# Rolling an 8192 x 8192 array by 100 columns: long memory-to-memory DMAs in 18 shrinking steps instead of 128 equal ones, and the row heads in four stages instead of two

## The chip, the cores and the metric

The kernel runs on one core of one Trainium2 chip. The metric is device time in microseconds (us), less is better.

## The reference

```python
def setup_inputs():
    return {"x": np.random.randn(8192, 8192).astype(np.float32), "shift": 100}

def reference(x, shift):
    return np.roll(x, shift, axis=1)
```

Nothing is computed. 268 MB are read and 268 MB are written, and each row of 32 KiB moves right by 400 bytes, with its last 100 columns coming round to the front.

## The kernel before

With a shift of 100, `s` is 100, `a` is 128 (the shift rounded up) and `g` is 28. The row from column 128 on, 8,064 elements or 32,256 bytes, is copied from memory to memory directly. Each DMA takes 16 rows, one for each of the 16 DMA engines, 4 rows (128 KiB) apart; SyncE and ScalarE issue them in turn:

```python
xm = x.rearrange("(c e j) w -> c j e w", e=16, j=4)
om = out.rearrange("(c e j) w -> c j e w", e=16, j=4)
for c in range(n_rows // 64):
    for j in range(4):
        engines[j % 2].dma_start(out=om[c, j, :, a:], in_=xm[c, j, :, g:n_cols - s])
```

The first 128 columns of each row, the heads, go through SBUF on GpSimd's queue. They are read in pieces of 512, 400 and 112 bytes, put together by VectorE, and written in pieces of 512 bytes:

```python
Q, J = 4, 8
n_st = n_rows // (P * Q * J)          # 2 stages
for k in range(n_st):
    ...                               # 3 + 1 + 1 reads, 2 copies
for k, h in enumerate(tiles):
    for q in range(Q):
        nc.gpsimd.dma_start(out=ot[k, q, :, :, :a], in_=h[:, q])
```

Of the kernel before, what the change touches and what calls it, by code (L numbers as in the profile page):

```python
# [1 line left out]

# [4 lines left out]


@with_exitstack
def kernel(  # L10
    ctx: ExitStack,
    tc: tile.TileContext,
    x: bass.AP,
    shift: int,
    out: bass.AP,
):
    nc = tc.nc
    n_rows, n_cols = x.shape
    s = shift % n_cols
    a = -(-s // 128) * 128  # L20
    g = a - s
    P = nc.NUM_PARTITIONS
    engines = [nc.sync, nc.scalar]
    n_chunks = 16
    rows = n_rows // n_chunks





    xm = x.rearrange("(c e j) w -> c j e w", e=16, j=4)
    om = out.rearrange("(c e j) w -> c j e w", e=16, j=4)
    if a < n_cols:
        for c in range(n_rows // 64):
            for j in range(4):
                engines[j % 2].dma_start(out=om[c, j, :, a:], in_=xm[c, j, :, g:n_cols - s])
    if a == 0:
        return


    if a > 512:
        for i in range(n_chunks):
            r = slice(i * rows, (i + 1) * rows)
            nc.gpsimd.dma_start(out=out[r, :s], in_=x[r, n_cols - s:])
            if g > 0:
                nc.gpsimd.dma_start(out=out[r, s:a], in_=x[r, :g])
        return





    Q, J = 4, 8
    n_st = n_rows // (P * Q * J)
    reads = ctx.enter_context(tc.tile_pool(name="reads", bufs=n_st))
    heads = ctx.enter_context(tc.tile_pool(name="heads", bufs=n_st))
    xt = x.rearrange("(k p j q) c -> k q p j c", q=Q, j=J, p=P)
    ot = out.rearrange("(k p j q) c -> k q p j c", q=Q, j=J, p=P)
    tiles = []
    for k in range(n_st):  # L60
        t = reads.tile([P, Q - 1, J, a], x.dtype)
        h = heads.tile([P, Q, J, a], x.dtype)
        for q in range(1, Q):
            lead = bass.AP(tensor=x.tensor, offset=(k * P * J * Q + q) * n_cols - s,
                           ap=[[J * Q * n_cols, P], [Q * n_cols, J], [1, a]])
            nc.gpsimd.dma_start(out=t[:, q - 1], in_=lead)  # L66
        nc.gpsimd.dma_start(out=h[:, Q - 1, :, :s], in_=xt[k, Q - 1, :, :, n_cols - s:])  # L67
        nc.vector.tensor_copy(h[:, :Q - 1, :, :s], t[:, :, :, :s])  # L68
        if g > 0:
            nc.gpsimd.dma_start(out=h[:, 0, :, s:], in_=xt[k, 0, :, :, :g])  # L70
            nc.vector.tensor_copy(h[:, 1:, :, s:], t[:, :, :, s:])  # L71
        tiles.append(h)
# [5 lines that stand above are left out]
# [1 line left out]
_INS = ['x', 'shift']  # L79
_OUTS = [((8192, 8192), 'float32')]  # L80

_NUMBERS = {'shift': 100}


# [26 lines left out]
```

## Time and profile before

| What | Before |
|---|---|
| time, median of 3 runs at first | 828.16 us |
| traffic, read and written | 268.44 MB each way |
| DMA engines' time: long rows, heads | 95.0%, 4.1% |
| long packets of 32,256 bytes | 8,192, and as many 4-byte completions (packets that report that an engine has finished its part of a DMA) |
| VectorE and GpSimd busy | 0% and 2% |

Everything is in the DMA rows: how full the 16 DMA engines are (DMA), and what they move (GB/s, in one direction). A long packet is the copy of one row by one engine. The prediction below shows the lines.

Numbers of single packets are worked out from the trace's packet records, which have queue, start, duration and size of each packet. "Memory traffic" counts a long packet's bytes twice, for read and write, and a head packet's bytes once, because its other side is SBUF. For before it is 657 GB/s from 300 to 500 us.

### The profile page before, as it was taken

To read this page: it belongs to the slowest core of one execution; us is meant where nothing else is said; L and a number is where in the kernel's file an instruction comes from. 1 tells how busy PE (TensorE), PEld (TensorE's weight loads), DVE (VectorE), ACT (ScalarE), POOL (GpSimd) and SP (SyncE) were. 2 spreads that over 40 slices of the span, in tenths; PEclk is the share of its full clock that TensorE was granted. 3 is DMA by queue.
4 is the path that set the end of the run, shared out by engine and by line. 5 is a ranking of instruction groups with operands and counts; after the bars stand their busy time and mean duration, and the time that the engine had idled before them with its cause. 6 is when DMAs were issued, how large, how long until landed. Compare 5 with 4: busy or idle time off the path is not lost. (4 is left out here: it accounts for less than half of the span.)

```text
span 826.9 us, 589 instructions
## 1 busy us (share of the span) xinstructions
DVE 3.7 (0%) x4; POOL 16.1 (2%) x22
## 2 busy tenths in 40 slices
DVE  0000000000000000000000000000000000000000
POOL 3001001000000000000000000000000000000000
DMA  9999999999999999999999999999999999999997
GB/s 305 336 338 333 337 344 351 347 352 343 339 342 330 329 329 321 334 329 326 326 328 325 337 329 325 340 318 329 317 336 333 330 325 326 328 326 339 321 328 261
DMA packets 18724, 272.70 MB, mean 330 GB/s; under 512 B 8480, under 2 KB 8480, under 8 KB 10528
## 3 DMA queue, kind: packets, MB, share of 16 engines
q10 hardware_dynamic: 8192, 132.14, 47.8%
q1 hardware_dynamic: 8192, 132.14, 47.2%
q0 software_dynamic: 2336, 8.39, 4.1%
q14 instruction: 4, 0.03, 0.0%
HBM read 268.44 MB, written 268.44 MB: 649 GB/s over the span
## 5 line engine op out<-in xcount | busy, mean ns | idle before, releaser
L75 POOL DMA_DIRECT2D out_dram<-h x8 | 6.9, 955 | 92.4 <-DMA h<-in_x_dram 79.9
L66 POOL DMA_DIRECT2D t<-in_x_dram x6 | 5.4, 910 | 0.8 <-PEq L106 0.8
L68 DVE COPY h<-t 128x2400 f32<-128x2400 f32 x2 | 2.8, 1410 | 116.2 <-DMA t<-in_x_dram 116.2
L67 POOL DMA_DIRECT2D h<-in_x_dram x2 | 1.8, 882 | 15.1 <-DMA t<-in_x_dram 15.1
L70 POOL DMA_DIRECT2D h<-in_x_dram x2 | 1.8, 883 | 14.4 <-DMA t<-in_x_dram 14.4
L71 DVE COPY h<-t 128x672 f32<-128x672 f32 x2 | 1.0, 504 | 0.0
L92 POOL MEMSET const-float32-0.0<- 128x1 f32 x1 | 0.1, 98 | 0.2 <-issue 0.2
L92 POOL MEMSET const-bfloat16-1.0<- 128x1 bf16 x1 | 0.1, 101 | 0.0
L92 POOL MEMSET const-float32-1.0<- 128x1 f32 x1 | 0.1, 98 | 0.0
L92 POOL MEMSET const-uint8-127<- 128x1 uint8 x1 | 0.1, 98 | 0.0
## 6 DMA issues: line engine op xcount, KB each, us to landing
out_dram<-in_x_dram ACTq DMA_DIRECT2D x256, 504.0 KB, 12.7
out_dram<-in_x_dram SPq DMA_DIRECT2D x256, 504.0 KB, 12.7
out_dram<-h POOLq DMA_DIRECT2D x8, 512.0 KB, 97.6
t<-in_x_dram POOLq DMA_DIRECT2D x6, 512.0 KB, 65.8
h<-in_x_dram POOLq DMA_DIRECT2D x2, 400.0 KB, 84.0
h<-in_x_dram POOLq DMA_DIRECT2D x2, 112.0 KB, 81.3
```

The costliest lines, as they stand in the source:

```text
L66: nc.gpsimd.dma_start(out=t[:, q - 1], in_=lead)
L67: nc.gpsimd.dma_start(out=h[:, Q - 1, :, :s], in_=xt[k, Q - 1, :, :, n_cols - s:])
L68: nc.vector.tensor_copy(h[:, :Q - 1, :, :s], t[:, :, :, :s])
L70: nc.gpsimd.dma_start(out=h[:, 0, :, s:], in_=xt[k, 0, :, :, :g])
L71: nc.vector.tensor_copy(h[:, 1:, :, s:], t[:, :, :, s:])
L75: nc.gpsimd.dma_start(out=ot[k, q, :, :, :a], in_=h[:, q])
L92: nc = _bacc.Bacc("TRN2", target_bir_lowering=False, num_devices=1)
```

## The change

Its intent is to have long transfers while there is much to do, to save issues and completions, and short ones at the end, so that the engines finish together. The heads go in smaller portions.

```diff
-    xm = x.rearrange("(c e j) w -> c j e w", e=16, j=4)
-    om = out.rearrange("(c e j) w -> c j e w", e=16, j=4)
-    if a < n_cols:
-        for c in range(n_rows // 64):
-            for j in range(4):
-                engines[j % 2].dma_start(out=om[c, j, :, a:], in_=xm[c, j, :, g:n_cols - s])
+    xm = x.rearrange("(c e j) w -> j e c w", e=16, j=4)
+    om = out.rearrange("(c e j) w -> j e c w", e=16, j=4)
+    blocks = n_rows // 64
+    steps, c = [], 0
+    while c < blocks:
+        steps.append((c, max(1, (blocks - c) // 4)))
+        c += steps[-1][1]
+    for c, n in steps:
+        ways = 2 if c >= blocks - 4 else 1
+        edge = [a + (n_cols - a) * k // ways for k in range(ways + 1)]
+        for j in range(4):
+            for lo, hi in zip(edge, edge[1:]):
+                if lo < hi:
+                    engines[j % 2].dma_start(out=om[j, :, c:c + n, lo:hi], in_=xm[j, :, c:c + n, lo - s:hi - s])
...
-    Q, J = 4, 8
+    Q, J = 4, 4
```

## The prediction

> **What bounds the kernel now.** I read the page first for the busy shares, then the stretches of the run (busy time and DMA share by window), then the waits of SyncE, then the waits of the other engines, and last the packet records of the trace. The page's parts 2 and 3 show that no compute engine matters and that the DMA engines are never free:
>
> ```profile
> DMA  9999999999999999999999999999999999999997
> GB/s 305 336 338 333 337 344 351 347 352 343 339 342 330 329 329 321 334 329 326 326 328 325 337 329 325 340 318 329 317 336 333 330 325 326 328 326 339 321 328 261
> q10 hardware_dynamic: 8192, 132.14, 47.8%
> q1 hardware_dynamic: 8192, 132.14, 47.2%
> q0 software_dynamic: 2336, 8.39, 4.1%
> HBM read 268.44 MB, written 268.44 MB: 649 GB/s over the span
> ```
>
> The reader is to see three things. The 16 DMA engines are full in every slice but the last; 95% of their time goes to the two queues of long row pieces (the part outside the first 128 columns), 4.1% to the heads; and the rate falls from about 343 GB/s to about 327 GB/s once the heads are done. The stretches say the same more sharply:
>
> ```profile
> 0.00:6.50 6.50, 0.00 (x0) 5.42 (x10) 1.00 0.68 239
> ...
> 120.00:250.00 130.00, 0.00 (x0) 3.47 (x4) 1.00 1.00 347
> 260.00:800.00 540.00, 0.00 (x0) 0.00 (x0) 1.00 1.00 328
> 800.00:820.00 20.00, 0.00 (x0) 0.00 (x0) 1.00 0.98 323
> 820.00:827.00 7.00, 0.00 (x0) 0.00 (x0) 1.00 0.30 124
> ```
>
> The last two columns are the DMA share and GB/s. From 6.5 to 820 us the share is 0.98 or more. Only the first 6.5 us (0.68) and the last 7 us (0.30) have idle DMA engines: 0.32 x 6.5 + 0.70 x 7 = 7 us of the 827, and no change of order can win more than that at the ends.
>
> Inside the full stretch an engine is busy but not at its best. In the packet records all 8192 long packets have 32,256 bytes. The shortest take 1,193 ns, 27 GB/s for an engine, 433 GB/s for 16; after 260 us the mean is about 1,555 ns and only 17% of packets are at the minimum. At the very end, from 821.7 us on, when fewer than 12 or so engines still have work, every packet takes 1,192 to 1,194 ns. So an engine is stretched by the others, not by its own work. Counting what HBM sees (twice the long bytes, once the heads' bytes, whose other side is SBUF), 20 us bins give 640 to 670 GB/s both while the heads' writes run (120 to 250 us) and after them. The common limit is thus **memory traffic at about 655 GB/s**, and 12 engines x 27 x 2 = 649 GB/s is just where the stretching stops. The traffic is 537 MB either way; 537 / 655 = 820 us.
>
> The waits of SyncE look alarming and are not:
>
> ```profile
> SPq L36 <- DMA out_dram<-in_x_dram: 679.2, 252, 6.0
> out_dram<-in_x_dram SPq DMA_DIRECT2D x256, 504.0 KB, 12.7
> ```
>
> The queue waits 679 us because only four DMAs per queue are allowed to be in flight, eight in all; each is one row per DMA engine and lands 12.7 us after its issue. 8 rows x 1.56 us = 12.5 us, so this is queueing behind work, not latency. The full DMA share shows that the window of eight is deep enough.
>
> **What the Trainium skill says.** (1) "DMA: Bandwidth & Descriptors", section on the anatomy of one DMA, gives about 2 us of fixed time for a DMA on the software path, and its section Bandwidth asks for 1 MiB or more per DMA. Here 504 KB DMAs run with a DMA share of 1.00, so that time lies beside other DMAs' data; larger DMAs have nothing of it to win. (2) The same page, section "Queues, rings and completion order", says that an engine takes turns between queues at packet granularity and that a completion is an ordered write behind earlier writes. The trace agrees with the turns (heads' packets lie between long ones) and shows the completions as 4-byte packets of 9 ns. (3) "HBM Reference", Specifications, gives some 716 GB/s for the pair's memory; 655 is 91% of that. The trace also shows more for an instant: the second round, from 3.98 us, has 16 packets in step at about 1,275 ns, 16 x 32,256 B / 1.275 us = 405 GB/s in each direction. So the limit depends on how the streams fall on each other, not only on bytes. (4) "DMA: Bandwidth & Descriptors", section "Latency and other measured facts", has copies slow down at row pitches of 512 KiB to 8 MiB. That bears on rival B below; no run here shows it yet.
>
> **The change part by part.**
>
> Larger DMAs. Each of 128 blocks has 64 rows, 4 per DMA engine. Steps of 32, 24, 18, 13, 10, 7, 6, 4, 3, 2, 2 blocks and seven of one replace 128 steps; the last four are cut into half rows. That is 14 x 4 + 4 x 8 = 88 DMAs for 512, with 124 x 64 + 4 x 128 = 8,448 long packets. Issues fall by 424 x 0.51 us (durations in the timeline), but SyncE and ScalarE are idle in waits, so this is worth 0. Completions fall from 8,192 to 88 x 16 = 1,408: 6,784 x 9 ns / 16 = **3.8 us of engine time**. If memory is the limit, the freed time only makes the other packets longer; I count a third, -1.3 us.
>
> Looser coupling. Eight DMAs in flight now mean up to some 200 rows per engine at first. In the present kernel, long packets plus their completions fill about 15.95 of 16 engines after 260 us, 0.3% idle; that bounds what waiting for the slowest engine costs at 0.3% x 820 = 2.5 us, and it again frees engines rather than memory: -0.5 us. The same number says that engines don't differ systematically by more than a few tenths of a per cent, since otherwise the fast ones would already stall.
>
> The start. The first DMA now carries 512 pieces instead of 16. The present first packets begin between 2.14 and 3.10 us after an issue at 0.74. If engines get their lists one after another they may start further apart: +0.5 us.
>
> The end. Now the engines finish between about 822.4 and 825.5 us, then 1.4 us of closing. With half rows the last packet is 0.6 us instead of 1.2. But engines that drifted apart during the long steps have to be brought together by the short ones: -0.8 us from the pieces, +1 us for drift.
>
> Heads. Four stages of 4 rows per partition: 12 + 4 + 4 reads and 16 writes, 36 DMAs for 18, each about 0.9 us of issue on GpSimd, 16 us more on an idle engine. The pieces are still 512, 400 and 112 bytes, so packets of about 4 KB stay about as many (2,048 now). The copies double in number with half the size (1.41 and 0.50 us now), on an idle engine. The heads end at 253 us of 827; even at half the speed they would be hidden. 0 us. The only trace of them should be 16 x 18 = 288 more completion packets of 9 ns, 0.2 us of engine time.
>
> Sum: -1.3 - 0.5 + 0.5 - 0.8 + 1 = about -1 us; I round to 826 from 828.16, since the parts lean down.
>
> **The rivals.** A: the ordered completion after every row stalls the engine, and this is the 360 ns between 1,193 and 1,555. For it: completions follow each row now, and all but a sixth would go. It could bring the mean packet near 1,300 ns and the time to 700 us. Against it: the rows of the second round (1,275 ns) and of the last 4 us (1,194 ns) also have a completion each. I give it 5%; a partial effect of 20 to 50 ns a row (-10 to -25 us) some 5% more.
>
> B: the new order hits memory worse. An engine used to step through neighbouring rows of one 2 MiB block; now its successive rows on a queue lie 2 MiB apart and engines can be in different blocks. For it: the skill's remark on row pitch. Against it: at one moment the 16 engines still stand 128 KiB apart as before, and their positions inside rows are already mixed. A 3% loss would give 850 us. 6%. It could as well turn out a gain of 1 to 3%.
>
> C: drift. Without a short leash an engine could end up 10 us behind, and the end would have fewer than 12 engines for that long: +3 to +6 us, 831 to 834. Against it: the 0.3% above, and packets of slow engines speed up to 1,193 ns as soon as others run dry. 15%, still within 2%.
>
> D: heads starved between long lists of rows, so that they end last. Against it: turns are by packet; they use a third of the run now. 2%.
>
> **Range and chances.** The bulk is set by bytes and a rate that I expect to hold within 1%: +-8 us; ends and drift add -2 to +5. So 817 to 836. Faster by over 2% (under 811.6) needs A or a lucky B: 0.09. Slower by over 2% (over 844.7) needs B or D: 0.07. Within 2%: 0.84.
>
> **What would show it.** Right: GB/s near 327 in the middle slices; mean long packet 1,540 to 1,570 ns; 1,400 or so completions on the two queues; heads over by 220 to 300 us; DMA share 1.00 until about 815 us. Wrong: a long-packet mean under 1,500 ns (A, or B as a gain), over 1,600 (B as a loss), a DMA share below 0.9 for over 10 us before the end (C), heads' packets in the last quarter (D). The prediction fails if the rate of the middle moves by more than 2%, in either direction, for then memory's rate is not a constant of this copy but depends on the order of rows or on completions.

## More of the kernel before

Times that are compared were taken on the same chip, beside runs of the kernel before. The experiments' profiles are not: the one trace of the kernel before was taken apart from them, and its medians differ by about 1% between chips (821 to 831 us), so a difference of 1% between such profiles means nothing by itself.

## The result, and the profile after

| | Before | Changed |
|---|---|---|
| median of 6 runs | 827.84 us | 828.95 us |
| range | 827.28 to 828.73 | 828.24 to 829.98 |
| ratio | | 1.0013 (95%: 1.0001 to 1.0026) |

A ratio is the mean time of one kernel's fast runs over that of the other's of the same rounds, so it is not quite the ratio of the medians. The two kernels take the same time; if anything the changed one is 1 us slower. The page of the changed kernel, parts 2 and 3 (40 slices of the span; then queue, packets, MB, share of the engines' time; q1 and q10 carry the long rows, q0 the heads):

```profile
DMA  9999999999999999999999999999999999999998
GB/s 312 323 344 322 337 338 327 337 339 331 332 332 331 327 337 337 339 335 338 338 341 333 335 339 338 317 326 329 325 329 331 325 331 331 323 323 323 331 312 296
q10 hardware_dynamic: 4928, 132.12, 47.6%
q1 hardware_dynamic: 4928, 132.12, 46.9%
q0 software_dynamic: 2624, 8.39, 4.1%
HBM read 268.44 MB, written 268.44 MB: 650 GB/s over the span
```

The two hardware queues have 9,856 packets instead of 16,384, because 6,784 completions are gone and 256 packets came from the half rows. The bytes, the shares and the GB/s stay. One thing has moved: the step down in the GB/s line, which marks the end of the heads, is after slice 25 (about 520 us) and no longer after slice 12 (about 250 us). In the packet records the last head packet with data ends at 521.5 us, before at 252.2 us.

The same stretches as before (us; then VectorE and GpSimd busy, clock, DMA share, GB/s):

```profile
0.00:6.50 6.50, 0.00 (x0) 5.41 (x11) 1.00 0.69 238
...
260.00:800.00 540.00, 0.00 (x0) 7.13 (x10) 1.00 0.99 331
800.00:820.00 20.00, 0.00 (x0) 0.00 (x0) 1.00 0.94 326
820.00:827.00 7.00, 0.00 (x0) 0.00 (x0) 1.00 0.58 184
```

The start is the same (238 against 239 GB/s). In the middle 331 stands against 328, because there are still heads in it; from 600 to 780 us, where neither kernel has any, memory traffic is 653 against 657 GB/s. Near the end the share is lower than before (0.94 against 0.98) and the rate is not (326 against 323). So idle DMA engines cost nothing in that stretch. The waits of SyncE and the issues show how far the DMAs grew (issues: count, KB each, median us from issue to landing):

```profile
SPq L44 <- DMA out_dram<-in_x_dram: 680.9, 40, 80.3
...
out_dram<-in_x_dram SPq DMA_DIRECT2D x2, 16128.0 KB, 159.2
...
out_dram<-in_x_dram SPq DMA_DIRECT2D x16, 252.0 KB, 6.0
```

SyncE waits 681 us in 40 waits, where it waited 679 us in 252. The issues that were saved were never on the path.

### The profile page after: what moved, and what is told of

It is laid out like the page before. It is cut to its first block, busy times and chain, and to the rows that moved or that the text cites. A ratio compares the mean times of both kernels' runs of the same rounds, so it can differ in the third digit from the quotient of the medians.

```text
span 826.3 us, 193 instructions
## 1 busy us (share of the span) xinstructions
DVE 4.5 (1%) x8; POOL 27.3 (3%) x40
## 3 DMA queue, kind: packets, MB, share of 16 engines
q0 software_dynamic: 2624, 8.39, 4.1%
## 5 line engine op out<-in xcount | busy, mean ns | idle before, releaser
L83 POOL DMA_DIRECT2D out_dram<-h x16 | 11.6, 726 | 217.2 <-DMA out_dram<-h 118.2
L74 POOL DMA_DIRECT2D t<-in_x_dram x12 | 9.5, 794 | 65.6 <-DMA h<-in_x_dram 36.1
L78 POOL DMA_DIRECT2D h<-in_x_dram x4 | 3.0, 749 | 47.1 <-DMA t<-in_x_dram 47.1
L76 DVE COPY h<-t 128x1200 f32<-128x1200 f32 x4 | 3.1, 785 | 253.8 <-DMA t<-in_x_dram 253.8
L75 POOL DMA_DIRECT2D h<-in_x_dram x4 | 3.0, 749 | 46.2 <-DMA t<-in_x_dram 46.2
L79 DVE COPY h<-t 128x336 f32<-128x336 f32 x4 | 1.7, 425 | 0.0
```

The source lines that it names most:

```text
L74: nc.gpsimd.dma_start(out=t[:, q - 1], in_=lead)
L75: nc.gpsimd.dma_start(out=h[:, Q - 1, :, :s], in_=xt[k, Q - 1, :, :, n_cols - s:])
L76: nc.vector.tensor_copy(h[:, :Q - 1, :, :s], t[:, :, :, :s])
L78: nc.gpsimd.dma_start(out=h[:, 0, :, s:], in_=xt[k, 0, :, :, :g])
L79: nc.vector.tensor_copy(h[:, 1:, :, s:], t[:, :, :, s:])
```

## The experiments

Twelve runs were made in three calls, each call on a chip of its own. The kernel before took 821.03, 831.28 and 831.33 us in them (medians), so times of different calls are not compared, only ratios.

The theory under test is the prediction's: memory traffic at some 655 GB/s sets the time, and neither the engines nor the issues do. The rivals are that the engines' time is the limit, that two effects cancel, and that completions, drift (engines that get ahead of one another when nothing holds them together) or the order of rows matter.

The late end of the heads gave a second theory to test, the turn theory: each DMA engine takes one packet from each queue in turn, and a completion packet uses up a turn just as a long packet does.

### First call: the parts alone, and what limits

**rows_only**: the changed kernel with the old heads.

```diff
-    Q, J = 4, 4
+    Q, J = 4, 8
```

> Only the tapering long-row DMAs of the change, heads in two stages as before. Memory theory (about 655 GB/s of memory traffic sets the time, whoever issues it): 828 to 830 us, within 0.3% of before. Cancelling theory (one part of the change wins what the other loses): off by 0.5% or more, most likely faster, since completions are fewer. Turn theory of the heads (every completion packet of 4 bytes takes a turn of its own among the queues, so one row per DMA gives the heads' queue a turn per long packet and many rows per DMA a turn per two): heads end near 500 us although their DMAs are those of before. If instead the four stages slow the heads: they end near 250 us.

Measured: 820.21 us against 821.03, ratio 0.9992 (0.9974 to 1.0010).

**heads_only**: the kernel before with the new heads.

```diff
-    Q, J = 4, 8
+    Q, J = 4, 4
```

> Only the four head stages of the change, long rows in 512 DMAs as before. Memory theory: 828 us within 0.3%. Cancelling theory: off by 0.5% or more, in the other direction than rows_only. Turn theory: heads end near 250 us as before, with about 0.9 head packets per long packet between 20 and 120 us. If the four stages slow the heads: they end near 520 us.

Measured: 826.17 us against 821.03, ratio 1.0057 (1.0033 to 1.0081). That is outside what the memory theory expected, and it was repeated in the third call.

Which part moved the end of the heads is seen in the GB/s lines of the two. First rows_only (818.1 us in 40 slices), then heads_only (825.1 us):

```profile
GB/s 303 331 332 342 329 345 334 336 331 345 342 338 340 344 339 338 344 344 339 345 340 341 343 328 331 334 330 333 325 336 326 334 328 330 325 333 333 330 323 286
```

```profile
GB/s 304 329 339 335 340 345 329 333 335 344 353 338 337 332 327 330 325 333 330 328 333 328 328 339 319 336 327 330 327 328 338 326 339 328 335 333 330 336 327 263
```

With the new rows and the old heads the step is after slice 23; the last head packet with data ends at 459.5 us. With the old rows and the new heads it ends at 284.7 us. So it is mainly the long-row DMAs that slow the heads. The turn theory expected that: 0.45 head packets with data per long packet in rows_only from 20 to 120 us, 0.84 in heads_only, 0.89 in before. The four stages add the rest, in the same way: they bring 288 completion packets of their own, so the heads' queue has 2,624 packets instead of 2,336, 12% more, and the heads end 13% later, both with the old rows (284.7 against 252.2 us) and with the new (521.5 against 459.5). Counted with these completions, from 5 us to the end of the heads, there are 0.98 head packets per long packet in before and heads_only, and 0.51 in rows_only and the changed kernel; turns alone would give 1 and 0.5.

**no_heads**: the kernel before, heads taken out. Its output is wrong, which doesn't matter for the time.

```diff
-    Q, J = 4, 8
-    n_st = n_rows // (P * Q * J)
... (all of the heads' code)
+    return
```

> The kernel before without any heads; the first 128 columns stay unwritten, so the result is wrong on purpose. The heads read and write 8.4 MB of memory together and take 4.1% of the DMA engines' time. Memory theory: 8.4 MB / 655 GB/s = 13 us less, 815 us. Engine-time theory (the 16 engines' occupancy bounds, long packets have a fixed duration): 4.1% of 827 = 34 us less, 794 us.

Measured: 805.97 us against 821.03, ratio 0.9811 (0.9787 to 0.9836), which is 15.5 us less (13.5 to 17.5). The page (queues, then HBM):

```profile
q10 hardware_dynamic: 8192, 132.14, 49.6%
q1 hardware_dynamic: 8192, 132.14, 49.5%
...
HBM read 264.24 MB, written 264.24 MB: 658 GB/s over the span
```

The engines' time that the heads had used was taken up again by the long packets, whose share rose from 95.0 to 99.1%, and HBM still ran at 658 GB/s. The engine-time theory (34 us) is out. The memory theory's 13 us is just under the interval; the rest may be that traffic in before was only 639 GB/s while heads were being read (20 to 120 us) against 657 later, 2.7% of 100 us. The trace of no_heads has no such dip (659 GB/s in that stretch, 662 later). That this makes up the rest is argued, not tested.

**write_only**: the long rows written from an SBUF tile, never read from memory. Its output is wrong, which doesn't matter for the time.

```diff
-        for c in range(n_rows // 64):
-            for j in range(4):
-                engines[j % 2].dma_start(out=om[c, j, :, a:], in_=xm[c, j, :, g:n_cols - s])
+    src = ctx.enter_context(tc.tile_pool(name="src", bufs=1)).tile([P, n_cols - a], x.dtype)
+    nc.sync.dma_start(out=src[:, :], in_=x[:P, g:n_cols - s])
+    for c in range(n_rows // P):
+        engines[c % 2].dma_start(out=out[c * P:(c + 1) * P, a:], in_=src[:, :])
... (and no heads)
```

> The same long rows are written, but from one SBUF tile instead of from memory, so memory sees 264 MB instead of 528; wrong on purpose, no heads. Memory theory: packets fall to the minimum of 1193 ns, 27 GB/s an engine, and the time to 264 MB / 433 GB/s = 610 us plus ends, 610 to 640 us. A theory in which each engine is slowed by its own copy work or by completions and not by memory: packets stay near 1500 ns and the time near 800 us.

Measured: 630.41 us, ratio 0.7679 (0.7664 to 0.7693). Its stretch from 20 to 600 us (GpSimd busy, clock, DMA share, GB/s):

```profile
20.00:600.00 580.00, 0.00 (x0) 1.00 1.00 431
```

The same 16 engines, just as full, move 431 instead of 328 GB/s, with a mean packet of 1,201 ns. A full DMA share thus did not mean that engines were the limit: some 360 ns of each long packet in before (1,559 less 1,201) are not the engine's own work. This run also changed the source from memory to SBUF, and loads alone were not measured; the copies at the end of no_taper, below, show the same without that change.

### Second call: the order of rows, and the shrinking

**near_rows** and **far_rows** change only which rows the 16 engines work on together.

```diff
-    xm = x.rearrange("(c e j) w -> c j e w", e=16, j=4)
-    om = out.rearrange("(c e j) w -> c j e w", e=16, j=4)
+    xm = x.rearrange("(c j e) w -> c j e w", e=16, j=4)     # near_rows: 32 KiB apart
+    om = out.rearrange("(c j e) w -> c j e w", e=16, j=4)
+    xm = x.rearrange("(e c j) w -> c j e w", e=16, j=4)     # far_rows: 16 MiB apart
+    om = out.rearrange("(e c j) w -> c j e w", e=16, j=4)
```

> The kernel before with one change: the 16 DMA engines copy 16 neighbouring rows (32 KiB apart) at a time instead of rows 128 KiB apart. If the memory rate of about 655 GB/s does not depend on the order of rows: within 0.5% of before. If it depends on how far apart the streams stand, it moves by over 2%, in a direction that I can't tell.

Measured: 839.54 us against 831.28, ratio 1.0093 (1.0055 to 1.0131): a little slower, between the two expectations.

> The kernel before with one change: each DMA engine has its own 512 rows, so that the 16 streams stand 16 MiB apart. Rate independent of order: within 0.5%. If streams at a large power of two fall on the same parts of memory, as rival B of the prediction has it, the rate of the middle falls and the time rises by 3% or more.

Measured: 2566.5 us (runs of 2587.38, 2553.15, 2579.84 and 2211.88), against 831.28. The fastest run is 2.66 times before's median. The page of a 2,587 us run:

```profile
DMA  9999999999999999999999999999999999999999
GB/s 113 107 114 107 109 113 111 118 117 113 114 109 104 104 99 102 100 112 97 104 104 99 104 109 102 98 102 108 101 103 100 100 107 106 101 101 99 112 104 92
```

The DMA engines are as full as ever and move a third; the mean long packet takes 4,766 ns (300 to 500 us). So the rate is no constant. Only the addresses were changed here, which speaks for memory itself as the shared limit and not the way to it; that is an inference. In the change, the 16 parts of a DMA still start 128 KiB apart.

**stripes**: the 16 engines share each row.

```diff
-        for c in range(n_rows // 64):
-            for j in range(4):
-                engines[j % 2].dma_start(out=om[c, j, :, a:], in_=xm[c, j, :, g:n_cols - s])
+        xs = x[:, g:n_cols - s].rearrange("(c r) (e w) -> c e r w", r=16, e=16)
+        os = out[:, a:].rearrange("(c r) (e w) -> c e r w", r=16, e=16)
+        for c in range(n_rows // 16):
+            engines[c % 2].dma_start(out=os[c], in_=xs[c])
```

> The kernel before with one change: the 16 DMA engines share each row, 2,016 bytes apiece, 16 rows in a DMA, so that all streams read one neighbouring 32 KiB. The pieces are 16 times as many. If memory traffic alone bounds and the engines have 20% to spare (1193 against 1555 ns), the cost of a piece is hidden: within 1%. If streams that walk together collide less, as in the second round of before (405 GB/s), faster by over 2%. If the fixed cost of a piece shows, slower by over 2%.

Measured: 879.48 us, ratio 1.0574 (1.0544 to 1.0605), slower. The smallest piece takes 80 ns; 2,016 bytes at 27 GB/s would be 75, so by this estimate about 5 ns are fixed. The mean is 104 ns, 1.3 times the minimum, as for whole rows (1,555 over 1,193 ns), but in another way: half of the pieces take 82 ns or less, and one in twenty over 165. So no gain from walking together shows. Whether the fixed part or the slow pieces made this kernel slower was not separated.

The run also bears on the turn theory. The heads' DMAs are those of before, and yet the heads are over after 67 us instead of 252, because the packets beside them are short. From 20 to 60 us there are 0.53 head packets (completions included) per piece; with one completion after 16 pieces, turns alone give 17/32 = 0.53.

**no_taper**: the changed kernel with four equal steps of 32 blocks, and so without half rows.

```diff
-        steps.append((c, max(1, (blocks - c) // 4)))
+        steps.append((c, 32))
```

> The changed kernel without its shrinking steps: four steps of 32 blocks, 16 long DMAs in all, so that nothing holds the engines together. Drift theory (rival C): engines drift apart by more than they do in the changed kernel, where up to one of 16 is idle from 660 us on; the end with fewer than 12 engines lasts several us and the time is 3 to 10 us above the changed kernel's, 831 to 840 us where before takes 828. No-drift theory: within 2 us of before. Memory theory in both: over 600 to 780 us the memory traffic is 650 to 665 GB/s and all 16 engines are busy.

Measured: 834.37 us against 831.28, ratio 1.0029 (1.0005 to 1.0053), 2.4 us. The last stretches of no_taper (829.1 us span in the profiled run):

```profile
780.00:800.00 20.00, 0.00 (x0) 0.00 (x0) 1.00 0.93 321
800.00:810.00 10.00, 0.00 (x0) 0.00 (x0) 1.00 0.90 310
810.00:820.00 10.00, 0.00 (x0) 0.00 (x0) 1.00 0.81 335
820.00:830.00 10.00, 0.00 (x0) 0.00 (x0) 1.00 0.34 148
```

The same stretches of the changed kernel:

```profile
780.00:800.00 20.00, 0.00 (x0) 0.00 (x0) 1.00 0.97 331
800.00:810.00 10.00, 0.00 (x0) 0.00 (x0) 1.00 0.89 326
810.00:820.00 10.00, 0.00 (x0) 0.00 (x0) 1.00 0.98 326
```

Engines do drift: about three of them have nothing left to do by 810 us, 18 us before the end. And yet the 13 others move 335 GB/s from 810 to 820, because their packets shorten to 1,269 ns on average (810 to 815 us). Sorted by how many engines were busy beside it, a long packet after 780 us takes on average 1,505 ns with 15 engines, 1,432 with 14, 1,271 with 13 and 1,194, the minimum, with 12. All of these are copies of one size from memory to memory, so the stretching comes from the other engines. This is why drift and the cure for it are both worth little: no_taper lost 2.4 us (0.4 to 4.4). Over the changed kernel that is about 1.3 us (1.0029 against 1.0013, not measured side by side); less than the 3 to 10 us expected.

### Third call: repeats, the turns, and another distance

**after_again** (the changed kernel, no edit) and **heads_again** (the edit of heads_only).

> The changed kernel once more, on the chip of the next three runs, to be compared with heads_again in the same rounds. On its first chip it took 1.0013 of before. Memory theory: 0.998 to 1.004 again, and the middle at 650 to 660 GB/s of memory traffic unless this chip's own rate differs.

Measured: 832.89 us against 831.33, ratio 1.0013 (0.9994 to 1.0032), the same ratio as on the first chip.

> heads_only once more: it was slower by 0.57% (0.33 to 0.81%) on its chip, which the memory theory did not expect, while rows_only was at 0.9992. If the four head stages do cost something when rows go one at a time: 1.003 to 1.008 again, and after_again below it. If that was a state of that chip or of placement: within 0.3% of before and of after_again.

Measured: 832.93 us, ratio 1.0031 (1.0006 to 1.0056), with runs from 831.91 to 838.2. Its interval reaches from almost nothing to what heads_only measured. Four stages beside one-row DMAs cost something, 0.1 to 0.8%; the cause is not settled. The traces give a lead: from 100 to 175 us memory traffic was 627 GB/s in heads_only and 630 in heads_again, against 661 and 653 in the same runs from 300 to 800 us. By estimate that is 3.8 and 2.7 us, a part of the 6.3 and 6.9 us by which these two profiled runs lie above before's median (the ratios give 4.7 and 2.6). The kernel before (654 and 657) and the changed one (653 and 655) have no such dip in that stretch. No run tested it.

**two_rows**: two rows per engine in each DMA, a test of the turn theory alone.

```diff
-    xm = x.rearrange("(c e j) w -> c j e w", e=16, j=4)
-    om = out.rearrange("(c e j) w -> c j e w", e=16, j=4)
+    xm = x.rearrange("(c e j) w -> j e c w", e=16, j=4)
+    om = out.rearrange("(c e j) w -> j e c w", e=16, j=4)
...
-        for c in range(n_rows // 64):
+        for c in range(0, n_rows // 64, 2):
...
-                engines[j % 2].dma_start(out=om[c, j, :, a:], in_=xm[c, j, :, g:n_cols - s])
+                engines[j % 2].dma_start(out=om[j, :, c:c + 2, a:], in_=xm[j, :, c:c + 2, g:n_cols - s])
```

> The kernel before with two rows per DMA engine in each DMA, 256 DMAs, so one completion packet per two long packets. Turn theory: two queues with 2 long packets and 1 completion each make 3 turns of the heads' queue per 4 long packets; counted against before (two turns per 2 long, measured 0.89) and rows_only (one per 2, measured 0.45) that is about 0.67 head packets per long packet between 20 and 120 us, and the heads end half way between 252 and 460 us, near 330 us. If the four or more rows in flight decide and not the completions: 0.89 or 0.45. Time within 0.5% of before.

Measured: 0.64 head packets with data per long packet (20 to 120 us), and the last of them ends at 332.9 us; 0.67 and about 330 were expected. From 5 us to the heads' end and with their completions it is 0.74, where turns alone give 0.75. With one, a half and (nearly) no completion per long packet the heads ended at 252, 333 and 460 us. The time of the single run, 838.46 us, is 0.9% above before's median of that chip; its state is unknown, so nothing is built on it, but it misses the 0.5%.

**odd_pitch**: streams 5 rows apart.

```diff
+        for lo, hi, j_n in ((0, 8160, 5), (8160, 8192, 2)):
+            xp = x[lo:hi].rearrange("(c e j) w -> c j e w", e=16, j=j_n)
+            op = out[lo:hi].rearrange("(c e j) w -> c j e w", e=16, j=j_n)
+            for c in range((hi - lo) // (16 * j_n)):
+                for j in range(j_n):
... (one DMA each, SyncE and ScalarE in turn)
```

> The kernel before with streams 5 rows (160 KiB) apart instead of 4 (128 KiB), no power of two. far_rows (16 MiB apart) fell to a third, near_rows (32 KiB) lost 0.9%. If a power of two costs something at 128 KiB too: faster by 1 to 5%, and this would beat both kernels. If 650 to 660 GB/s is what reading and writing at once can have at any small pitch: within 0.7% of before.

Measured: 842.19 us against 831.33, ratio 1.0136 (1.0111 to 1.0161). It is slower, so against 160 KiB, the one other distance tried that is no power of two, 128 KiB loses nothing. Of the distances tried, 32 KiB, 128 KiB, 160 KiB and 16 MiB, the one of both kernels is the best. No version that beats both was found.

## Why the prediction was right

The time, 828.95 us, lies in the range of 817 to 836 and within 2% of before, as was held likeliest. Point by point:

- **The bound.** Right: no_heads took 15.5 us off where the bytes said 13 and the engines' time 34, write_only ran the same engines at 431 GB/s, and in no_taper copies are stretched when more than 12 engines are busy, as the prediction's 12 x 27 x 2 = 649 GB/s has it. A limit that the engines share is shown. That it lies in the memory is argued from far_rows, which also shows that its size depends on the order of rows.
- **Completions, -1.3 us, and coupling, -0.5 us.** All 6,784 completions went, as counted, and 88 x 16 = 1,408 stayed. rows_only, which has both terms along with start and end, gave -0.7 us with an interval of -2.1 to +0.8. A small gain is possible and none is shown.
- **Start, +0.5 us.** It was 0: the first packets begin between 2.22 and 2.86 us, before between 2.14 and 3.10. A list of 512 pieces does not start the engines one after another.
- **End and drift, -0.8 and +1 us.** The last data land at 825.0 us in the profiled run, before at 825.5. Drift came, more than I thought: from 660 us on between 0.3 and 1 of 16 engines is idle. The sign that I gave, a DMA share of 1.00 until 815 us, failed (0.97 from 780 to 800 us, 0.89 from 800 to 810). It did not matter, for the reason that no_taper shows.
- **Heads, 0 us.** This is the step that failed in its working. I expected their end between 220 and 300 us, since packets stay as many and turns go by packet. It was 521.5 us. I had counted only long packets as turns; the 4-byte completions are turns too, and with those of the rows went half of the heads' turns (459.5 us with the new rows alone). The heads' own 288 more completions, counted as 0.2 us of engine time, are turns as well and made the rest. The safety margin in the same sentence (half the speed would still be hidden) is what saved the number. Alone, the four stages measured +0.3 to +0.6% rather than 0; in the changed kernel at most a part of that is left. It may be why the change measured +1 us where the sum said -1, but the dip that goes with it is not in the changed kernel's trace, and the cause is open. A sum of five terms of about 1 us each could not settle the sign.
- **The rivals.** A is out: with five sixths of the completions gone the long packet takes 1,545 ns from 600 to 780 us, where neither kernel has heads, before 1,562. B names a real mechanism that the change does not touch: far_rows lost two thirds, but in the changed kernel only the rows that follow each other on one engine are 2 MiB apart, and rows_only shows that to be harmless. C happened and was cheap; its sign (a DMA share below 0.9 for over 10 us) was on the edge, with 0.89 from 800 to 810 us. D did not, although the heads came closer to it (521 of 826 us) than the prediction allowed.

## What to carry to other kernels

Where every DMA engine is full, ask what stretches the packets: compare the mean packet with the shortest, and count bytes at the memory. If memory is the limit, as in this copy, larger DMAs, fewer completions and idle engines near the end are worth next to nothing, while the distance between the streams that run together can cost a factor of three. And a queue beside others gets its share by packets, tiny completions included, so merging one queue's DMAs slows its neighbour; check that the neighbour has the time.

## What the Trainium skill lacked or had wrong

- "DMA: Bandwidth & Descriptors", Queues, rings and completion order, has turns at packet granularity and does not say that a completion packet takes a turn of its own. Here 0.98, 0.74 and 0.51 head packets (their own completions included) came per long packet with 1, 1/2 and nearly no completions for each, and the heads ended at 252, 333 and 460 us.
- The same page, Latency and other measured facts, gives row pitches of 512 KiB to 8 MiB with a loss of about half at most, for tiles of 16 KiB rows, from a full 214 GB/s per direction. For a memory-to-memory copy of 32 KiB rows, 16 streams 16 MiB apart had 103 to 112 GB/s against 328 at 128 KiB, a third. Distances of 32 and 160 KiB cost 0.9 and 1.4%.
- The same page's advice of 1 MiB or more per DMA gained nothing in this copy with eight DMAs in flight: 504 KB and up to 16 MB per DMA took the same time (rows_only 0.9992).
- "HBM Reference" has no figure for reading and writing at once. Here it is 650 to 660 GB/s in sum, while writes alone ran at 431, limited by the engines.
- No page was found that says how much chips differ: the same kernel took 821.0 us on one and 831.3 us on two others (medians).
